# Rotary embedding on the first half of each head: a tile loaded as 11 and 5 rows instead of 8 and 8, and a store released one instruction earlier

## The chip, the core and the metric

The kernel runs on one core of one Trainium2 chip. The metric is device time of one execution in microseconds (us), the median over runs. Three runs of the kernel before were timed: 161.6, 161.76 and 161.9 us. Beside them stands one profiled execution of the same kernel, from which all durations in this text come.

## What is computed

The input `x` has the shape 16 x 512 x 16 x 64 (batch, sequence, heads, dim), in float32: 33.55 MB. `cos` and `sin` are tables of 512 x 32. Of the 64 numbers of a head only the first 32 change, and of the tables only the first 16 columns are used:

```
x1, x2 = x[..., :32], x[..., 32:]
rotated_first  = x1[..., :16] * cos[..., :16] - x1[..., 16:] * sin[..., :16]
rotated_second = x1[..., :16] * sin[..., :16] + x1[..., 16:] * cos[..., :16]
out = concatenate([rotated_first, rotated_second, x2], axis=-1)
```

The second half of each head is copied as it is. So all 33.55 MB are read from HBM and 33.55 MB are written.

## The kernel before, in words

**Tiles.** The 8192 rows of `x` (one row is a batch and sequence position, 16 heads x 64 numbers, 4 KB) are cut into four tiles of 128 partitions x 16 rows: a partition holds 64 KB of a tile, and a whole tile is 8.39 MB. In the code `K` is 16, `KC` is 8 (half a tile) and `KM` is 5. The tiles live in `ring`, which has three slots (`NS`), so tile 3 takes the slot of tile 0 and its load must wait until the store of tile 0 has landed. A tile is loaded into its slot, changed in place and stored from there; the half that isn't rotated travels along.

**Tables.** `cos` and `sin` come by two small DMAs from GpSimd's queue (L63, L64); VectorE spreads them to all partitions (L73 to L83).

**Compute.** All arithmetic is on VectorE. `rotate(t, lo, hi)` works on the rows lo to hi of tile t with four instructions: a product with sin into `b_t` (L96), a product with cos in place (L97), a subtraction for the first 16 columns (L98) and an addition for the second 16 (L101). The tiles are done in order; tile 0, 1 and 3 in two calls of 8 rows; tile 2 as rows 8 to 16, then 0 to 5, then 5 to 8.

**Queues.** The order of transfers is written out by hand. SyncE's queue (SP) issues, in this order: load of tile 0, load of tile 1, load of rows 8 to 16 of tile 2, store of tile 0, load of rows 0 to 8 of tile 2, load of tile 3, store of tile 1, store of tile 3. Only the store of tile 2 is issued by GpSimd (POOL). An instruction of SP that waits holds back those behind it. In what follows "store(0)" is the store of tile 0, and so on; "the first part" and "the second part" of tile 2 are its two loads in their order in time (rows 8 to 16 and rows 0 to 8 here).

**The added wait.** store(1) doesn't wait for tile 1 alone. A dependency added by hand (`tc.add_manual_dep`) lets it wait also for `near`, the last instruction of `rotate(2, 0, KM)`, that is the addition L101 of the rows 0 to 5 of tile 2.

The lines `load` L55 and `store` L58 are helpers, so every load has the line L55 and every store L58 in the profile.

Of the kernel before, what the change touches and what calls it, by code (L numbers as in the profile page):

```python
# [1 line left out]

# [4 lines left out]


@with_exitstack
def kernel(  # L10
    ctx: ExitStack,
    tc: tile.TileContext,
    x: bass.AP,
    cos: bass.AP,
    sin: bass.AP,
    out: bass.AP,
):
    nc = tc.nc
    fp32 = mybir.dt.float32
    P = 128  # L20
    B, S, H, D = x.shape
    Q = D // 4
    HF = D // 2

    K = 16
    T = B * S // (P * K)
    PB = S // K
    REP = P // PB  # L30
    R = H * D
    NS = 3
    KC = K // 2
    KM = 5

    xf = x.rearrange("b s h d -> (b s h d)").rearrange("(t p f) -> t p f", t=T, p=P)
    of = out.rearrange("b s h d -> (b s h d)").rearrange("(t p f) -> t p f", t=T, p=P)
    cosf = cos.rearrange("(p k) j -> p (k j)", k=K)
    sinf = sin.rearrange("(p k) j -> p (k j)", k=K)

    const_pool = ctx.enter_context(tc.tile_pool(name="const", bufs=1))
    b_pool = ctx.enter_context(tc.tile_pool(name="bp", bufs=1, space=bass.MemoryType.PSUM))


    ring = const_pool.tile([P, NS, K, H, D], fp32)
    stage = const_pool.tile([P, 2, K, HF], fp32)
    spun = const_pool.tile([P, 2 * K, Q], fp32)
    packed = const_pool.tile([PB, 2 * K, Q], fp32)
    table = const_pool.tile([P, 2, K, 2, Q], fp32)

    def rows(t, lo, hi):
        return ring[:, t % NS, lo:hi].rearrange("p k h d -> p (k h d)")

    def load(t, lo=0, hi=K):
        return nc.sync.dma_start(out=rows(t, lo, hi), in_=xf[t, :, lo * R : hi * R])  # L55

    def store(t, lo=0, hi=K, queue=nc.sync):
        return queue.dma_start(out=of[t, :, lo * R : hi * R], in_=rows(t, lo, hi))  # L58


    nc.vector.memset(stage[:, :, :, 0:Q], 0.0)  # L61
    spread = stage.rearrange("(j b) t k i -> j b t (k i)", b=REP)
    nc.gpsimd.dma_start(out=spread[:, 0, 0], in_=cosf)  # L63
    nc.gpsimd.dma_start(out=spread[:, 0, 1], in_=sinf)  # L64
    load(0)
    load(1)
    load(2, KC, K)

    PQ = PB // REP
    nc.vector.stream_shuffle(  # L73
        out=spun[:],
        in_=stage.rearrange("p t k j -> p (t k) j")[:, :, 0:Q],
        mask=[j % PQ * REP for j in range(PB)],
    )
    for q in reversed(range(REP)):
        n = PQ * (q + 1)
        nc.vector.tensor_copy(out=packed[0:n], in_=spun[q * PB : q * PB + n])  # L80

    for r in range(REP):
        nc.vector.tensor_copy(  # L83
            out=table[r * PB : (r + 1) * PB].rearrange("p t k c j -> p (t k) c j"),
            in_=packed.unsqueeze(2).to_broadcast((PB, 2 * K, 2, Q)),
        )
    C = table[:, 0].rearrange("p k c j -> p k (c j)")
    Sn = table[:, 1].rearrange("p k c j -> p k (c j)")

    def rotate(t, lo, hi):  # L90
        x1 = ring[:, t % NS, lo:hi, :, 0:HF]
        c = C[:, lo:hi].unsqueeze(2).to_broadcast((P, hi - lo, H, HF))
        s = Sn[:, lo:hi].unsqueeze(2).to_broadcast((P, hi - lo, H, HF))
        b_full = b_pool.tile([P, KC, H, HF], fp32, name="b_t")
        b_t = b_full[:, 0 : hi - lo]
        nc.vector.tensor_mul(out=b_t, in0=x1, in1=s)  # L96
        nc.vector.tensor_mul(out=x1, in0=x1, in1=c)  # L97
        nc.vector.tensor_sub(  # L98
            out=x1[:, :, :, 0:Q], in0=x1[:, :, :, 0:Q], in1=b_t[:, :, :, Q:HF]
        )  # L100
        return nc.vector.tensor_add(  # L101
            out=x1[:, :, :, Q:HF], in0=x1[:, :, :, Q:HF], in1=b_t[:, :, :, 0:Q]
        )

    rotate(0, 0, KC)
    rotate(0, KC, K)
    store(0)
    load(2, 0, KC)
    load(3)
    rotate(1, 0, KC)  # L110
    rotate(1, KC, K)
    behind_loads = store(1)
    rotate(2, KC, K)
    near = rotate(2, 0, KM)
    rotate(2, KM, KC)
    store(2, queue=nc.gpsimd)

    tc.add_manual_dep(
        behind_loads.ins,
        near.ins.name,  # L120
        mybir.DependencyInfo(mybir.DependencyClass.Sync, mybir.DependencyReason.DATA),
        reason="the store follows the loads at the DMA engines",
    )
    rotate(3, 0, KC)
    rotate(3, KC, K)
    store(3)


# [1 line left out]
_INS = ['x', 'cos', 'sin']  # L130
_OUTS = [((16, 512, 16, 64), 'float32')]


# [23 lines left out]
```

## Time and profile before

| what | value | where from |
| --- | --- | --- |
| median of three timed runs | 161.76 us (161.6 to 161.9) | the times |
| span of the profiled execution, first to last instruction | 159.5 us | the page's first line |
| outside of that span, by the median | 2.3 us | 161.76 - 159.5 |
| VectorE (DVE) busy | 112.9 us, 71% of the span | part 1 of the page |
| moved by DMA | 67.24 MB, 422 GB/s over the span | part 2 and 3 |
| HBM read and written | 33.69 MB and 33.55 MB | part 3 |

The profiled execution isn't among the timed ones and has no time of its own beside its span, so the 2.3 us around the span are the difference to the median, taken as unchanged by the edit.

How to read it: the page gives shares of the span; the timeline lists instructions with start and duration, DMA issues among them (an engine name with a q behind it is the engine's sequencer, which issues); the view by windows gives, for any stretch of time, the busy time of each engine, the granted TensorE clock, the DMA share and the GB/s. In this last view a DMA packet (the piece of one partition's row, up to 64 KB, that one of the 16 DMA engines moves) counts with its whole duration and size at its start. So a stretch can show a share over 1, or 0 while all 16 engines work; a stretch in which 16 packets start and that is about one packet long shows a share near 1. The share times the length of the stretch is the time those packets took, per engine.

### The profile page before, as it was taken

The page shows a single profiled execution, that of the slowest core. Times are in us where ns is not written, and L with a number is a line of the kernel's source. Part 1 is how long each engine was busy: PE and PEld are TensorE (multiplying, and loading weights), DVE is VectorE, ACT ScalarE, POOL GpSimd, SP SyncE. Part 2 cuts the span into 40 slices and gives each one's busy share as a digit, 9 for nine tenths or more (in the row PEclk, how much of TensorE's full clock was granted, in tenths as well). Part 3 has the DMA queues.
Part 4 walks back from the last instruction along what each step waited for, and adds up shares of the span by engine and source line. Part 5 has one row for each costly group of instructions (what it writes and reads, how often), then busy time and mean ns, then how long its engine had stood idle before and what let it go on. Part 6 is the DMA issues. An engine that isn't in the chain of part 4 may idle for free.

```text
span 159.5 us, 115 instructions
## 1 busy us (share of the span) xinstructions
DVE 112.9 (71%) x47; POOL 1.9 (1%) x7
## 2 busy tenths in 40 slices
DVE  1000959999999999999999999999999990000000
POOL 3000000000000000000000000010000000000000
DMA  7969979799699699699996996996996997999966
GB/s 263 542 263 542 444 345 526 345 444 526 271 493 551 279 510 526 263 394 411 510 526 263 526 526 263 526 526 263 526 526 263 526 460 329 526 394 394 526 263 263
DMA packets 1360, 67.24 MB, mean 422 GB/s; under 512 B 176, under 2 KB 176, under 8 KB 208
## 3 DMA queue, kind: packets, MB, share of 16 engines
q1 hardware_dynamic: 1152, 58.72, 85.7%
q0 software_dynamic: 208, 8.52, 12.4%
HBM read 33.69 MB, written 33.55 MB: 422 GB/s over the span
## 4 chain that ended last, share of the span: by engine, by line
DVE 61%; DMA 14%; issue 5%; DVEq 1%
DVE b_t L96 22%; DVE ring L97 22%; DMA ring<-in_x_dram 14%; DVE ring L101 10%; DVE ring L98 7%; DVEq L152 1%; DVEq L96 0%
## 5 line engine op out<-in xcount | busy, mean ns | idle before, releaser
L96 DVE TENSOR_TENSOR b_t<-ring,table 128x4096 f32<-128x4096 f32 (+2 forms) x9 | 35.6, 3959 | 2.1 <-DMA ring<-in_x_dram 1.8
L97 DVE TENSOR_TENSOR ring<-ring,table 128x4096 f32<-128x4096 f32 (+2 forms) x9 | 35.5, 3950 | 0.3
L98 DVE TENSOR_TENSOR ring<-ring,b_t 128x2048 f32<-128x2048 f32 (+2 forms) x9 | 18.4, 2049 | 0.3
L101 DVE TENSOR_TENSOR ring<-ring,b_t 128x2048 f32<-128x2048 f32 (+2 forms) x9 | 18.4, 2043 | 0.0
L73 DVE LOAD_MASK_SELECT spun<-stage x1 | 0.0, 14 | 14.4 <-DMA stage<-in_sin_dram 14.4
L83 DVE COPY table<-packed 32x1024 f32<-32x1024 f32 x4 | 2.7, 684 | 0.1
L58 POOL DMA_DIRECT2D out_dram<-ring x1 | 0.6, 562 | 101.7 <-DVE ring L101 101.7
L80 DVE COPY packed<-spun 32x512 f32<-32x512 f32 (+3 forms) x4 | 1.7, 416 | 0.1
L61 DVE MEMSET stage<- 128x512 f32 x1 | 0.5, 485 | 0.9 <-PEq L141 0.9
L73 DVE STREAM_SHUFFLE spun<-stage 128x512 f32<-128x512 f32 x1 | 0.7, 721 | 0.0
L63 POOL DMA_DIRECT2D stage<-in_cos_dram x1 | 0.6, 644 | 1.3 <-DVE stage L61 1.3
L64 POOL DMA_DIRECT2D stage<-in_sin_dram x1 | 0.5, 535 | 0.0
L141 POOL MEMSET const-bfloat16-1.0<- 128x1 bf16 x1 | 0.1, 102 | 0.0
L141 POOL MEMSET const-float32-0.0<- 128x1 f32 x1 | 0.1, 99 | 0.2 <-issue 0.2
L141 POOL MEMSET const-float32-1.0<- 128x1 f32 x1 | 0.1, 99 | 0.0
L141 POOL MEMSET const-uint8-127<- 128x1 uint8 x1 | 0.1, 99 | 0.0
## 6 DMA issues: line engine op xcount, KB each, us to landing
ring<-in_x_dram SPq DMA_DIRECT2D x2, 4096.0 KB, 40.7
stage<-in_cos_dram POOLq DMA_DIRECT2D x1, 64.0 KB, 9.0
stage<-in_sin_dram POOLq DMA_DIRECT2D x1, 64.0 KB, 13.3
ring<-in_x_dram SPq DMA_DIRECT2D x3, 29.0
out_dram<-ring SPq DMA_DIRECT2D x3, 27.4
out_dram<-ring POOLq DMA_DIRECT2D x1, 39.5
```

Source lines behind the costliest of these rows:

```text
L58: return queue.dma_start(out=of[t, :, lo * R : hi * R], in_=rows(t, lo, hi))
L61: nc.vector.memset(stage[:, :, :, 0:Q], 0.0)
L63: nc.gpsimd.dma_start(out=spread[:, 0, 0], in_=cosf)
L64: nc.gpsimd.dma_start(out=spread[:, 0, 1], in_=sinf)
L73: nc.vector.stream_shuffle(out=spun[:], in_=stage.rearrange("p t k j -> p (t k) j")[:, :, 0:Q], mask=[j % PQ * REP for j in range(PB)],)
L80: nc.vector.tensor_copy(out=packed[0:n], in_=spun[q * PB : q * PB + n])
L83: nc.vector.tensor_copy(out=table[r * PB : (r + 1) * PB].rearrange("p t k c j -> p (t k) c j"), in_=packed.unsqueeze(2).to_broadcast((PB, ...
L96: nc.vector.tensor_mul(out=b_t, in0=x1, in1=s)
L97: nc.vector.tensor_mul(out=x1, in0=x1, in1=c)
L98: nc.vector.tensor_sub(out=x1[:, :, :, 0:Q], in0=x1[:, :, :, 0:Q], in1=b_t[:, :, :, Q:HF])
L101: return nc.vector.tensor_add(out=x1[:, :, :, Q:HF], in0=x1[:, :, :, Q:HF], in1=b_t[:, :, :, 0:Q])
L152: with _tile.TileContext(nc) as tc:
```

## The change

Three things are edited.

1. Tile 2 is loaded as rows 5 to 16 (11 rows, before the first store on SP's queue) and rows 0 to 5 (5 rows, behind it). Before, it was rows 8 to 16 and rows 0 to 8.
2. Rows 0 to 8 of tile 2 are rotated as rows 3 to 8 and then rows 0 to 3. Before, it was 0 to 5 and then 5 to 8. The pieces have 5 and 3 rows in both kernels.
3. `rotate` now returns its subtraction and not its addition, so `near`, for which store(1) waits, is the subtraction of rows 3 to 8 of tile 2. The addition follows it on VectorE as before.

```
-    KM = 5
+    KA = 5
+    KM = 3
...
-    load(2, KC, K)
+    load(2, KA, K)
...
-        nc.vector.tensor_sub(
+        first_half = nc.vector.tensor_sub(
...
-        return nc.vector.tensor_add(
+        nc.vector.tensor_add(
             out=x1[:, :, :, Q:HF], in0=x1[:, :, :, Q:HF], in1=b_t[:, :, :, 0:Q]
         )
+        return first_half
...
     store(0)
-    load(2, 0, KC)
+    load(2, 0, KA)
     load(3)
...
-    near = rotate(2, 0, KM)
-    rotate(2, KM, KC)
+    near = rotate(2, KM, KC)
+    rotate(2, 0, KM)
     store(2, queue=nc.gpsimd)
```

No instruction is added or removed on any engine, and each queue issues its transfers in the same order as before. In the changed file each line of `rotate`, `load` and `store` stands one line later (L55 is L56, L98 is L99, L101 is L102).

## The prediction

> **What bounds the kernel now.** I read the page first. VectorE is busy 71% of the span, the DMA row is near full in all but the last slices, and the two DMA queues together hold the 16 engines for 85.7 + 12.4 = 98.1% of the span.
>
> ```profile
> span 159.5 us, 115 instructions
> DMA  7969979799699699699996996996996997999966
> q1 hardware_dynamic: 1152, 58.72, 85.7%
> q0 software_dynamic: 208, 8.52, 12.4%
> DVE 61%; DMA 14%; issue 5%; DVEq 1%
> ```
>
> The last line is the chain that ended last. It runs through VectorE up to the issue of store(3) at 131.2 us, and reads as if VectorE set the end. It does not: store(3) is issued while older stores still keep the DMA engines busy. So the next thing to read is the view by windows around each handover from one transfer to the next, with the issues from the timeline beside it.
>
> ```profile
> 49.92 0.35 SPq L58 DMA_DIRECT2D out_dram<-ring  x1
> 50.31 0.43 SPq L55 DMA_DIRECT2D ring<-in_x_dram  x1
> 71.72 0.33 SPq L55 DMA_DIRECT2D ring<-in_x_dram  x1
> 95.99 1.49 DVE L98 TENSOR_TENSOR ring<-ring,b_t 128x1280 f32<-128x1280 f32 x1
> 97.39 1.48 DVE L101 TENSOR_TENSOR ring<-ring,b_t 128x1280 f32<-128x1280 f32 x1
> 98.90 0.34 SPq L58 DMA_DIRECT2D out_dram<-ring  x1
> ```
>
> These are store(0), the second part of tile 2, load(3), the subtraction and addition before store(1), and store(1).
>
> ```profile
> 1.74:2.60 0.86, 0.00 (x0) 0.86 (x2) 1.00 3.68 1219
> 47.20:49.60 2.40, 2.40 (x2) 0.00 (x0) 1.00 1.01 437
> 50.70:53.10 2.40, 2.40 (x1) 0.00 (x0) 1.00 1.01 437
> 53.10:55.50 2.40, 2.37 (x2) 0.00 (x0) 1.00 1.01 437
> 67.60:70.00 2.40, 2.37 (x2) 0.00 (x0) 1.00 1.15 437
> 70.00:72.50 2.50, 2.47 (x2) 0.00 (x0) 1.00 1.00 419
> 99.50:101.90 2.40, 2.37 (x2) 0.00 (x0) 1.00 1.01 437
> 157.60:159.50 1.90, 0.00 (x0) 0.00 (x0) 1.00 0.00 0
> ```
>
> Columns: the stretch, its length, busy VectorE and GpSimd, clock, DMA share, GB/s. 437 GB/s x 2.40 us is 1.05 MB: 16 packets of 64 KB, one on each engine. In the middle of a transfer (53.10) they take 1.01 x 2.40 = 2.42 us each, so 16 rows of a tile (8 packets an engine) take 19.4 us.
>
> With this the whole span can be added up. 67.1 MB of tiles are 64 packets per engine: 64 x 2.42 = 154.9 us. The tables (0.13 MB) are 0.3 us at the same rate. The first packets take 3.68 x 0.86 = 3.16 us instead of 2.42: 0.7 more. The last packets of store(0) take 1.15 x 2.40 = 2.76 us (0.34 more) and the first of the load behind it 1.00 x 2.50 = 2.50 per 64 KB (0.08 more): a turn from store to load that costs 0.42 us. From a start at about 1.9 us this gives 1.9 + 154.9 + 0.3 + 0.7 + 0.4 = 158.2 us, and the span ends at 159.5 us after the last landing. Nothing is left over for another hole. **The DMA engines bound the kernel, without a gap from the first packet to the last**, and all that can be won at handovers is the 0.42 us.
>
> **The change part by part.**
>
> *The load of 11 rows.* Same bytes in another order. The first part grows by 3 rows: 3/16 of 19.4 = 3.63 us more on the engines ahead of store(0), and 3.63 us less behind it. Sum on the engines: 0. Packets become 44 KB and 20 KB instead of 32 KB, as many as before. Packets of 32 KB run at the rate of 64 KB (the stretch 47.20, in the first part of tile 2, has 1.01 and 437 like the stretch 53.10). 20 KB isn't in the trace; at a loss of 1% on these 6.05 us it would be 0.06 us. I bound it at 0 to +0.1 us and take 0.
>
> What moves: store(0) is still issued at 49.92 us, since tile 0's arithmetic doesn't change, but its turn comes 3.63 us later, at about 54.6 instead of 51.0 us. It is thus queued 4.7 us ahead of its first packet instead of 1.1. It ends 3.63 us later; load(3), which waits on SP for its landing, is issued at 71.72 + 3.63 = 75.3 us. The second part of tile 2 covers this: it is now 5 rows, 6.05 us instead of 9.7, and ends at the old time, about 80.9 us, so load(3) is issued 5.6 us ahead of its turn. Without that cover each us would cost one us. Behind load(3) on SP stand only store(1) (97.5 us) and store(3) (131.2 us), so nothing else is delayed.
>
> VectorE's needs: rows 8 to 16 of tile 2 are used at 76.82 us and land at about 55.7 instead of 52; rows 3 to 8 are used at 90.26 us and the second part lands at 81.3 us as before (issue 50.31 plus 31.0 to landing); tile 3 is used at 104.36 us and lands at 71.72 + 29.0 = 100.7 as before. The nearest of these has 3.6 us to spare. Cost: 0.
>
> *Order 3 to 8, then 0 to 3.* The same shapes in the same places (5 rows, then 3): 0. store(2) on GpSimd waits for the last addition of tile 2, at 104.6 us in both.
>
> *The earlier release of store(1).* The subtraction ends at 95.99 + 1.49 = 97.48 us; the addition ends at 98.87 and the store is issued at 98.90. So store(1) is issued 1.4 us earlier, at 97.5 us. Its turn on the engines is when load(3) ends, from 99.9 us on. What is won is the hole at this handover, and the stretch at 99.50 shows none: 1.01, as in the middle of a transfer. The two decimals of the share allow 0.01 x 2.40 = 0.02 us. Gain 0 to 0.02; behind store(1) on SP nothing is due before 131.2 us. store(2) from GpSimd and store(3) mix with it or follow it on the same busy engines, so the end at about 158.2 us stays.
>
> *How close the cover is.* It matters whether the handovers at 51.0 and 99.9 us have no hole by a wide or a narrow margin. The trace has one start with nothing ahead of it: load(0), issued at 0.74 us. No packet starts before 1.74, and all 16 first packets start from 1.74 to 2.60 us, 1.0 to 1.86 us after the issue.
>
> ```profile
> 0.74:1.74 1.00, 0.48 (x1) 0.03 (x1) 1.00 0.00 0
> 98.90:99.80 0.90, 0.89 (x1) 0.00 (x0) 1.00 0.00 0
> 99.80:100.30 0.50, 0.50 (x1) 0.00 (x0) 1.00 4.86 2097
> ```
>
> store(1)'s 16 first packets start 0.9 to 1.4 us after its issue at 98.90, just when the engines become free. The cover is as long as the delay; a delay of 1.86 us would have left up to 1.86 - 1.0 = 0.9 us of hole. So before the edit both handovers stand at the edge, after it they have 4.7 and 2.4 us. In the profiled execution that is worth 0; in a timed one that falls on the wrong side of the edge it is worth 0 to 0.9 us at each.
>
> Here a rule can be weighed. The Trainium skill, "DMA: Bandwidth & Descriptors", section "Latency and other measured facts", puts the first byte of a transfer issued from SyncE at about 600 ns; the row here is 1.0 to 1.86 us, and the row decides. By the page's figure both handovers would have 0.3 us or more to spare, an earlier issue would be worth nothing in any run, and the sum would be 161.76 us.
>
> *A store queued early behind a load.* This is the state that the trace of before doesn't hold: store(0) issued 4.7 us ahead of its turn, before the engines begin the load's last packets. There is one turn with the following transfer queued long ahead, store(0) to the second part of tile 2 (issued at 50.31, its turn at 70.8 us), and it cost 0.42 us. The two turns from load to store, issued 1.0 us ahead, cost nothing. So the new one costs between 0 and +0.42 us, and from below -0.42 us if the old turn becomes cheaper. I take 0, by the rows with the same direction. store(1), issued at 97.5 us, is only 2.4 us ahead, about one packet: nearer to the rows of 0.
>
> **Sum**: 0 (bytes) + 0 (VectorE) - 0.02 to 0 (store(1)) + 0 (turns) = 159.5 us of span, and with 2.3 us around it 161.7 to 161.8 us. I forecast 161.7 us.
>
> **Rivals.**
> - *Slower: an early store spoils its turn.* If what costs at 70 us is not the direction but that the next transfer lies ready while the last packets run, so that it fetches data beside them, store(0) now pays the same: +0.42, 162.2 us; if store(1) pays too, 162.6 us. For it: the dear turn is the only one queued long ahead. Against it: load to load handovers are queued as long ahead and show no such stretch. It decides once the lead is over one packet, 2.42 us, which store(0) passes and store(1) just reaches. Chance 0.22, and 0.03 more for small packets or another mishap of the same size.
> - *Faster: the timed runs have the holes that the profiled one just misses.* Both handovers are on the edge; 0.4 to 0.5 us at one or both gives 161.3 to 160.8 us. For it: delays up to 1.86 us at load(0). Against it: packets follow without a hole at both handovers here. Chance 0.18.
> - *Faster: the dear turn gets cheaper* as the load behind store(0) has smaller packets: -0.42, 161.3 us. Nothing in the trace speaks for it. Chance 0.04.
> - *The edit does not do what it says*: it moves only what is covered. That is my forecast, chance 0.53.
>
> **Numbers.** A difference of 0.2% (0.32 us) is about what a measurement of this kernel can tell from no change. Faster 0.18 + 0.04 = 0.22, same 0.53, slower 0.22 + 0.03 = 0.25. The likeliest case by itself runs from 161.45 to 162.05 us. The range goes to 161.1 (one hole of 0.65 us closed) and to 162.4 us (one dear turn, and half of another); left out are two full holes and two full dear turns, with about 0.2.
>
> **What would show it.** Right: store(0) issued at 49.9 with its first packets at 54.6; load(3) issued near 75.3; store(1) issued at 97.5; shares near 1.01 at both load to store handovers; the last packets ending near 158.2. Wrong: a share over 1.1 around 54.6 or 99.9 us (early store), or a last packet clearly before or after 158.2 with no such stretch.

## The result and the profile after

The changed kernel takes 162.23 us (median of 6 runs, 162.01 to 163.04); the kernel before took 161.62 us (median of 6 runs, 161.27 to 161.90). The ratio is 1.0045, with a 95% interval of 1.0027 to 1.0062: **slower by 0.45%**. The profiled execution of the changed kernel took 162.12 us with a span of 160.0 us, so what lies around the span is 2.1 us, and the change is inside it: 160.0 against 159.5 us. (The 2.3 us taken for the kernel before came from two different runs; in e1 below one and the same run of it has 161.56 us and a span of 159.5 us, 2.1 us too.)

The page of the changed kernel looks like the one of before:

```profile
span 160.0 us, 115 instructions
DMA  7969979979889969969996996996996997998983
q1 hardware_dynamic: 1152, 58.72, 85.7%
q0 software_dynamic: 208, 8.52, 12.3%
```

The same packets take 85.7 + 12.3 = 98.0% of 160.0 us, which is 156.8 us per engine; before it was 98.1% of 159.5 us, 156.5 us. So most of the 0.5 us is packets that became longer, and not engines that stand idle (a tenth of a per cent is 0.16 us, so the page gives this sum no finer). The timeline of the changed kernel shows the issues (store(0), second part of tile 2, load(3), store(1)):

```profile
49.91 0.35 SPq L59 DMA_DIRECT2D out_dram<-ring  x1
50.30 0.44 SPq L56 DMA_DIRECT2D ring<-in_x_dram  x1
76.24 0.33 SPq L56 DMA_DIRECT2D ring<-in_x_dram  x1
97.50 0.34 SPq L59 DMA_DIRECT2D out_dram<-ring  x1
```

store(0) and store(1) are issued when the prediction said, load(3), which waits for store(0) to land, 0.9 us later than it said (75.3). The view by windows, with each stretch holding the start of one packet per engine, shows where the time is (for the 44 KB packets of the 11 rows, 1.66 us is the time at full rate: 44/64 of 2.42):

```profile
44.40:46.20 1.80, 1.77 (x2) 0.00 (x0) 1.00 0.99 400
46.20:48.00 1.80, 1.80 (x2) 0.00 (x0) 1.00 1.00 400
53.00:54.70 1.70, 1.67 (x2) 0.00 (x0) 1.00 1.32 424
55.30:57.70 2.40, 2.40 (x1) 0.00 (x0) 1.00 1.01 437
72.20:74.60 2.40, 2.37 (x3) 0.00 (x0) 1.00 1.01 437
74.60:75.40 0.80, 0.80 (x1) 0.00 (x0) 1.00 0.97 410
97.40:99.80 2.40, 2.37 (x3) 0.00 (x0) 1.00 1.01 437
```

Three things are to be seen. The **last packets of the 11 rows**, ahead of store(0), take 1.32 x 1.70 = 2.24 us instead of 1.66: 0.58 us too long. Two earlier rounds of 44 KB packets take 0.99 x 1.80 = 1.78 and 1.80 us: 0.26 us too long together. And the turn from store(0) to the load behind it (72.20 and 74.60), which cost 0.42 us before, is now free: 1.01 and 0.97 x 0.80 = 0.78 us where a 20 KB packet takes 0.76. The sum is 0.58 + 0.26 + 0.02 - 0.42 = +0.44 us; the span grew by 0.5. The last 0.1 us is not located. store(1)'s turn (97.40) is at full rate.

### The profile page after: what moved, and what is told of

It reads as the page before. It is cut to its first block, busy times and chain, and to the rows that moved or that the text cites. A ratio compares the mean times of both kernels' runs of the same rounds, so it can differ in the third digit from the quotient of the medians.

```text
span 160.0 us, 115 instructions
## 1 busy us (share of the span) xinstructions
DVE 112.9 (71%) x47; POOL 1.9 (1%) x7
## 3 DMA queue, kind: packets, MB, share of 16 engines
q1 hardware_dynamic: 1152, 58.72, 85.7%
q0 software_dynamic: 208, 8.52, 12.3%
## 4 chain that ended last, share of the span: by engine, by line
DVE 61%; DMA 14%; issue 5%; DVEq 1%
DVE b_t L97 22%; DVE ring L98 22%; DMA ring<-in_x_dram 14%; DVE ring L102 10%; DVE ring L99 7%; DVEq L154 1%; DVEq L97 0%
## 5 line engine op out<-in xcount | busy, mean ns | idle before, releaser
L98 DVE TENSOR_TENSOR ring<-ring,table 128x4096 f32<-128x4096 f32 (+2 forms) x9 | 35.6, 3950 | 0.3
L99 DVE TENSOR_TENSOR ring<-ring,b_t 128x2048 f32<-128x2048 f32 (+2 forms) x9 | 18.4, 2049 | 0.3
L102 DVE TENSOR_TENSOR ring<-ring,b_t 128x2048 f32<-128x2048 f32 (+2 forms) x9 | 18.4, 2043 | 0.0
```

The costliest lines, as they stand in the source:

```text
L99: first_half = nc.vector.tensor_sub(out=x1[:, :, :, 0:Q], in0=x1[:, :, :, 0:Q], in1=b_t[:, :, :, Q:HF])
L102: nc.vector.tensor_add(out=x1[:, :, :, Q:HF], in0=x1[:, :, :, Q:HF], in1=b_t[:, :, :, 0:Q])
```

## The experiments

All ratios are to the kernel before, run beside it on the same chip, with 95% intervals. A "round" is 16 packets, one per engine. "Excess" is a round's time in the view by windows less its time at full rate (2.42 us for 64 KB). The "lead" of a store is the time from its issue to the start of the last packets of the load ahead of it. Theories have letters; those that came up later are told in the expectation in which they first stand.

Theory A: a store that lies ready in the queue well ahead of its turn stretches the last packets of the load before it. Rivals: B, packets of 44 KB are slow by themselves; C, chance disturbances; D, the earlier store(1) costs.

**e1 and e2: both kernels again, unchanged.**

> The kernel before, run again, for a second trace. Theory A (a transfer that lies ready behind another of the other direction stretches that one's last packets): the last packets of store(0), from 68 us on, are again 0.3 to 0.4 us longer than 2.42 us, at the same place, and nothing else is long. Theory C (the long packets are chance disturbances of the memory that fall anywhere): the long packets stand elsewhere or are missing. Time: 161.6 us in both, ratio 1.000 within 0.002.

> The changed kernel, run again. Theory A: the last packets of the 11 rows, from 53.3 us on, are again 0.5 to 0.6 us longer than 1.67 us, and the turn at 74.9 us is free again. Theory B (packets of 44 KB are slow by themselves): the packets from 43 to 48.5 us take about 1.8 us again, 0.3 us in all. Theory C: neither comes back at its place. Time by A and B: ratio about 1.004; by C within 0.002 of 1 or scattered.

e1: 161.54 us, ratio 0.9999 (0.9990 to 1.0008). e2: 162.05 us, ratio 1.0035 (1.0022 to 1.0047). In e1 the last packets of store(0) are again long (share 1.17 where it was 1.15); in e2 the last packets of the 11 rows are:

```profile
52.90:54.60 1.70, 1.67 (x2) 0.00 (x0) 1.00 1.33 424
```

That is an excess of 0.60 us at the same place (0.58 in the first trace of the changed kernel), and the two rounds at 44.4 to 48 us have shares of 0.96 and 1.00 (0.2 us). C falls: the long packets belong to the program.

**e3 and e4: each part of the change alone.** e3 has the loads of 11 and 5 rows and the new order of the pieces, and store(1) waits for the addition (the edit is against the changed kernel):

```
-        first_half = nc.vector.tensor_sub(
+        nc.vector.tensor_sub(
...
-        nc.vector.tensor_add(
+        return nc.vector.tensor_add(
...
-        return first_half
```

e4 has the kernel before with only the subtraction returned:

```
+        first_half = nc.vector.tensor_sub(
...
+        return first_half
```

> The loads of 11 and 5 rows alone; the second store waits for the addition as before. Theory A and B: the whole loss stays, ratio 1.003 to 1.005, with last load packets of 2.2 us at 53 to 56 us. Rival D (the earlier issue of the second store is what costs): ratio within 0.001 of 1.

> The earlier release of the second store alone; loads of 8 and 8 rows. Theory A and B: ratio within 0.001 of 1, the issue of the second store at 97.5 us and no long packet at 99.9 us. Rival D: ratio 1.003 to 1.005, long packets at the end of load(3), 97.5 to 100.5 us.

e3: 162.15 us, ratio 1.0035 (1.0023 to 1.0048). e4: 161.79 us, ratio 1.0012 (1.0003 to 1.0021). The view by windows of e3, then of e4:

```profile
52.90:54.60 1.70, 1.67 (x2) 0.00 (x0) 1.00 1.48 424
```

```profile
67.60:70.00 2.40, 2.37 (x2) 0.00 (x0) 1.00 1.24 437
97.20:99.60 2.40, 2.37 (x3) 0.00 (x0) 1.00 1.04 437
```

The split alone has the whole loss (excess 0.86 us here; its 44 KB rounds at 44.4 to 48 us have shares of 0.94 and 0.96, only 0.1 us too long together). D falls as the main cause. But e4 isn't quite free, as A had expected: store(1), issued at 97.68 us, stretches the last packets of load(3) by 1.04 x 2.40 - 2.42 = 0.08 us. In its trace the old turn is longer too, 0.56 us instead of 0.34 in store(0)'s last packets, but that excess lies between 0.27 and 0.41 us in e1, e5, e10 and e11, which have the same rows ahead of this turn, so a part of it may be chance.

**e5 and e10: a store that lies ready much earlier, in the kernel before.** e5 leaves the added wait out, so store(1) is issued at 76.72 us; e10 waits for an earlier piece, and issues it at 90.27 us. e5, then e10:

```
-    tc.add_manual_dep(behind_loads.ins, near.ins.name, ...)
```

```
-    rotate(2, KC, K)
-    near = rotate(2, 0, KM)
+    near = rotate(2, KC, K)
+    rotate(2, 0, KM)
```

> The kernel before without the added wait: store(1) is issued at about 76.8 us, 23 us ahead of its turn behind load(3). Nothing else is changed. Theory A1 (each turn from load to store whose store lies ready before the last load packets start costs 0.5 to 0.8 us): the last packets of load(3), from 97.5 us on, are 0.5 us or more longer than 2.42, and the ratio is 1.003 to 1.005. Theory A2 (only the first turn with a transfer lying ready costs, about 0.4 to 0.6 us in all, wherever it stands): no long packet at 97.5 us, the one at 68 us stays, ratio within 0.001 of 1.

> The kernel before, with store(1) waiting for rows 8 to 16 of tile 2 instead of rows 0 to 5: it is issued at about 90.3 us, 7 us (three packets) ahead of the last packets of load(3), between the kernel before (98.9 us) and the one without the wait (76.7 us, 1.17 us lost). Step: the last packets of load(3) are again 1.1 to 1.2 us too long, ratio 1.005 to 1.007. Price by the lead: 0.5 to 0.9 us, ratio 1.002 to 1.004.

e5: 162.48 us, ratio 1.0062 (1.0049 to 1.0075). e10: 162.86 us, ratio 1.0083 (1.0069 to 1.0097). The last packets of load(3) in e5, then in e10:

```profile
97.10:99.50 2.40, 2.37 (x3) 0.00 (x0) 1.00 1.50 437
```

```profile
97.10:99.50 2.40, 2.37 (x3) 0.00 (x0) 1.00 1.51 437
```

Both are 1.2 us too long (1.50 x 2.40 = 3.60), where the kernel before has none; in e5 that is more than the 0.5 to 0.8 us expected, and A2 (only the first turn costs) falls. Nothing else differs from the kernel before but the moment of one issue, so this is theory A by itself: 14 us more of lead cost no more, so the price doesn't grow with the lead out here. It also tells what the added wait is for. The time of e10 is above its expected 1.005 to 1.007, though its stretch is no longer than that of e5; why is open.

**e6: the change's loads with store(0) held back.** The 11 and 5 rows stay; store(0) waits for a product that ends when the last load packets start (`rotate` also returns its products for that):

```
+    at_turn = rotate(1, 0, 6)[0]      # the product with sin
+    rotate(1, 6, KC)
...
+    tc.add_manual_dep(first_store.ins, at_turn.ins.name, ...)
```

> The changed kernel with its loads of 11 and 5 rows, but store(0) is held back until about 53.3 us, when the last load packets start, by a wait for a product of tile 1 (whose first call is cut into 6 and 2 rows for that). Theory A1: the long packets at 53.3 us go from 0.6 to under 0.1 us; the turn from store(0) to the load behind it, at 75 us, then costs 0.4 us as in the kernel before; the 44 KB packets at 45 to 48 us stay long (0.2 us); ratio about 1.001 to 1.002. If only what lies ready counts at any turn (theory A as it was), the same. If the turn at 75 us stays free, its cost in the kernel before came from its packets of 32 KB, and the ratio is about 0.999. Rival E (the place, not the lead, makes the last packets long): still 0.6 us at 53.3 us, ratio 1.004.

```profile
46.20:48.00 1.80, 1.80 (x2) 0.00 (x0) 1.00 1.01 400
52.90:54.60 1.70, 1.67 (x2) 0.00 (x0) 1.00 0.99 424
71.50:73.90 2.40, 2.37 (x2) 0.00 (x0) 1.00 1.03 437
```

store(0) is issued at 53.24 us, and the stretch ahead of it is gone (0.99 x 1.70 = 1.68 us); the slow 44 KB packets at 46 us stay. So the lead, and not the place or the packets' size, makes the last packets long. The turn at 73 us costs 0.05 us, where A1 had expected 0.4. The profiled execution has a span of 159.4 us, but the times scatter: 161.65 us (161.25 to 163.32, 12 runs), ratio 1.0021 (0.9997 to 1.0044). Ten runs lie between 161.25 and 162.13 us, two at 163.2 and 163.3. By its time e6 is inconclusive.

**e7: no packets of 44 KB.** The 11 rows are loaded by two DMAs:

```
-    load(2, KA, K)
+    load(2, KA, KC)
+    load(2, KC, K)
```

> The changed kernel, with its 11 rows loaded by two DMAs of 3 rows (12 KB packets) and 8 rows (32 KB packets), so that no packet has 44 KB; store(0) lies ready as early as in the changed kernel. Theory B (packets of 44 KB are slow by themselves): the 0.2 us at 45 to 48 us go. Theory A1: the last packets ahead of store(0) are still 0.5 us or more too long, so the ratio is 1.002 to 1.003 where the changed kernel has 1.004. Rival F (the stretch at the turn belongs to 44 KB packets too): no stretch, ratio below 1.001.

```profile
45.50:46.70 1.20, 1.17 (x1) 0.00 (x0) 1.00 1.01 437
53.30:54.60 1.30, 1.26 (x2) 0.00 (x0) 1.00 1.53 403
```

The 32 KB packets at 45 us run at full rate; the last ones ahead of store(0) take 1.53 x 1.30 = 1.99 us instead of 1.21, an excess of 0.78 us. This agrees with B on the 0.2 us, and F (the stretch belongs to 44 KB packets) falls. The time, 162.50 us, ratio 1.0057 (1.0045 to 1.0069), is above the expected 1.002 to 1.003. The stretch is 0.2 us larger than in the changed kernel, but that only makes up for the 0.2 us won at 45 to 48 us; where the other 0.3 us are wasn't found.

**e8: the load behind store(0) held back**, in the kernel before, until the last packets of store(0) have started.

```
+    at_turn = rotate(1, KC, 13)[1]
+    rotate(1, 13, K)
...
+    tc.add_manual_dep(second_part.ins, at_turn.ins.name, ...)
```

> The kernel before, with the second load of tile 2 held back until about 69.1 us, when the last packets of store(0) have started (tile 1's second call is cut into 5 and 3 rows for that, and store(1) waits for the subtraction of 6 rows, at about 99.0 us). Theory A (what lies ready stretches the last packets of the transfer before): the 0.4 us at 68 to 71 us go, ratio 0.997 to 0.998. Theory G (the 0.4 us are the time that the first reads of a load need behind a store, which a later issue can't shorten): they stay 0.4 us or grow, as a hole instead of long packets, ratio 1.000 to 1.003.

```profile
67.60:70.00 2.40, 2.37 (x2) 0.00 (x0) 1.00 1.01 437
70.00:72.60 2.60, 2.56 (x3) 0.00 (x0) 1.00 1.16 403
```

Issued at 69.10 us, the load no longer stretches the packets of store(0) (1.01), but its own first two rounds take 1.16 x 2.60 = 3.02 us instead of 2.42: 0.60 us lost instead of 0.42. Theory A as it stood ("of the other direction", either way) falls. G (the first reads of a load behind a store need this time) is right that a later issue saves nothing, though the time shows as long packets and not as the hole that G expected. **The two turns are not alike**: in the kernel before and in e8, time is lost from store to load whether the load lies ready or not; from load to store, it is lost only if the store lies ready early. The time, 161.94 us, ratio 1.0023 (1.0015 to 1.0032), holds also a store(1) issued at 99.49 instead of 98.90 us: its first packets start after 100.3 us, where the kernel before had them start from 99.8 to 100.3.

**e9, e17 and e18: the lead in steps.** The changed kernel with KA = 7, 6 and 4, that is 9, 10 and 12 rows ahead of store(0).

```
-    KA = 5
+    KA = 7        # e9; 6 in e17, 4 in e18
```

> The changed kernel with 9 and 7 rows instead of 11 and 5: the turn to store(0) comes 1.2 us later than in the kernel before instead of 3.6 us, so store(0) lies ready less than one packet of 36 KB (1.36 us) before the last packets start. Theory A1 with a step (any store that lies ready before the last packets start costs the whole 0.6 us or more): last load packets 0.6 us too long, ratio 1.003 to 1.004. Theory A1 with a price by the lead (0.6 us at 3.5 us ahead of the last packets, 1.2 us at 21 us): 0.1 to 0.3 us, ratio 1.000 to 1.002. The packets of 36 KB show whether only 44 KB is slow: 0 or about 0.1 us at 41 to 50 us.

> The changed kernel with 10 and 6 rows: store(0) is issued about 1.9 us ahead of the last load packets (40 KB, 1.5 us each), between 9 rows (0.8 us ahead: no stretch) and 11 rows (3.6 us ahead: 0.6 us). Price that grows with the lead: the last packets before store(0) are 0.2 to 0.4 us too long, ratio 1.001 to 1.003. Step at about one packet of lead: 0.6 us or more, ratio 1.003 to 1.004.

> The changed kernel with 12 and 4 rows: store(0) is issued about 4.7 us ahead of the last load packets (48 KB, 1.8 us each). Price that levels off at half the time of a last packet, as the 1.2 us of the 64 KB packets of load(3): 0.8 to 0.95 us, ratio 1.004 to 1.006. Price of 0.6 us whatever the size: 0.6 us, ratio 1.003 to 1.004.

The last packets of the first part, in e9 (36 KB, 1.36 us at full rate), e17 (the last two rounds, 40 KB, 1.51 us) and e18 (48 KB, 1.81 us):

```profile
50.40:51.80 1.40, 1.40 (x1) 0.00 (x0) 1.00 0.98 421
69.00:71.40 2.40, 2.40 (x1) 0.00 (x0) 1.00 1.04 437
```

```profile
50.20:51.70 1.50, 1.50 (x1) 0.00 (x0) 1.00 1.46 437
52.10:53.70 1.60, 1.60 (x1) 0.00 (x0) 1.00 1.23 410
```

```profile
53.70:55.60 1.90, 1.87 (x2) 0.00 (x0) 1.00 1.55 414
```

| kernel | store issued | last load packets start, about | excess ahead of the store |
| --- | --- | --- | --- |
| before, store(0) | 49.92 us | 50.1 us | 0 |
| e6, store(0) | 53.24 us | 53.5 us | 0 |
| e4, store(1) | 97.68 us | 97.8 us | 0.08 us |
| after, store(1) | 97.50 us | 98.1 us | 0 |
| e9, 9 rows | 50.04 us | 51.3 us | 0 |
| e17, 10 rows | 49.80 us | 52.9 us | 1.1 us, over two rounds |
| after, e2, e3, 11 rows | 49.9 us | 53.5 us | 0.58, 0.60, 0.86 us |
| e7, 3 and 8 rows | 50.04 us | 53.9 us | 0.78 us |
| e18, 12 rows | 50.04 us | 54.3 us | 1.1 us |
| e10, store(1) | 90.27 us | 97.5 us | 1.2 us |
| e5, store(1) | 76.72 us | 97.5 us | 1.2 us |

e17: 162.53 us, ratio 1.0061 (1.0046 to 1.0076). e18: 162.47 us, ratio 1.0057 (1.0040 to 1.0074). e9's last load packets start from 51.1 to 51.7 us (none starts from 50.32 to 51.08), so its lead is 1.3 us and not the 0.8 us of the expectations. It is a **step**: up to 1.3 us of lead, about one packet of e9, costs at most 0.08 us; 3.1 us and more cost 0.6 to 1.2 us. No run lies between (of e17's 3.1 us, 0.7 are its own stretch in the round before). So no run tells whether the step sits at a packet's length or at the delay from issue to first packet, which was 0.9 to 1.86 us in the kernel before. Above the step the price follows neither the lead nor the packet's size (0.78 us at 32 KB, 1.1 at 40 KB, 0.6 at 44 KB). So e9 (0) and e18 (1.1 us) lie outside both values that were expected for each, and why the change's own 11 rows get off cheapest stays open.

e9 has neither cost in its trace: nothing ahead of store(0), and 1.04 x 2.40 - 2.42 = 0.08 us at the turn to load. Yet its runs spread from 161.37 to 163.61 us (median 161.82), ratio 1.0033 (1.0012 to 1.0055).

**e11 and e12: can both turns be made cheap?** e11 loads the 8 rows behind store(0) as 5 and 3 rows; e12 is e6 with the 11 rows loaded as 3 and 8 (the edit of e7).

```
-    load(2, 0, KC)
+    load(2, 0, KM)
+    load(2, KM, KC)
```

> The kernel before, with the 8 rows behind store(0) loaded by two DMAs of 5 rows (20 KB packets) and 3 rows (12 KB). Theory H (the turn from store to load is cheap where the load's packets are small, as at 75 us in the changed kernel and in the one with a late store(0)): the 0.35 us at 68 to 72 us fall under 0.1 us, ratio 0.998. Theory I (it is cheap there because of what came ahead of it, not because of its packets): 0.3 to 0.5 us stay, ratio 1.000 to 1.001.

> The kernel with the late store(0) at about 53.2 us, its 11 rows loaded by DMAs of 3 and 8 rows: neither 44 KB packets nor an early store. Theories A1, B and H together: no stretch over 0.1 us at any turn, 0.2 us less at 45 to 48 us than with 44 KB packets, ratio 0.997 to 0.999, the best of all. If a further DMA costs something by itself, up to 1.001.

e11: 161.97 us, ratio 1.0033 (1.0021 to 1.0045). The last packets of store(0) are still 0.27 us too long, so H (small packets make this turn cheap) falls, and I (what came ahead makes it cheap) is left:

```profile
67.90:70.30 2.40, 2.40 (x1) 0.00 (x0) 1.00 1.12 437
```

The time of e11 is above what either expected (1.001 at most); its trace, of a run of 161.77 us, doesn't show why.

e12: 163.16 us (161.66 to 163.82), ratio 1.0088 (1.0055 to 1.0121), the worst and not the best. Its ten runs fall into two groups, four from 161.66 to 161.97 us and six from 162.92 to 163.82; the trace is of a 161.73 us run and shows no stretch at 53 us (share 1.01 over 1.20 us).

**e13 to e16: the kernels with long runs once more**, e12's (e13, e14), e9's (e15) and e6's (e16), one run each.

> The kernel of e12 (late store(0), 3 and 8 rows) once more. Its runs lay in two groups, near 161.7 and near 163.5 us, and the trace at hand is of the first. If this one is of the second group: theory J (store(0) sometimes still lies ready before the last load packets start, and stretches them) shows its 1.8 us as long packets at 53 to 56 us; theory K (the small packets of the first part stall) at 42 to 45 us; theory L (a hole at another turn) at 75 or 99 us.

> The kernel of e12 once more, as in e13, to have a trace of each of its two groups; theories J, K and L expect the same of it as there.

> The kernel of e9 (9 and 7 rows) once more; its runs spread from 161.4 to 163.6 us and the trace at hand is of a short one (161.6). Theory J: in a longer run the excess is in the last packets of 36 KB, at 50.5 to 53 us. Theory L: at another turn.

> The kernel of e6 (late store(0), 11 and 5 rows) once more; two of its 12 runs were near 163.2 us, the others near 161.6. Short: as e6, no stretch at 53.3 us. Long: by J the stretch is back at 53.3 to 56 us, by L it stands at another turn.

They took 161.68, 161.85, 161.66 and 161.68 us: all are short. What the 1.8 us of the long runs are is not known, and theories J, K and L stay untested.

No version beats the kernel before: of the kernels timed with an interval none lies below 1 with it.

## Why the prediction was wrong, point by point

- **The bound held.** The DMA engines have work from first to last packet in both kernels, and VectorE's waits moved nothing.
- **The step that failed is "a store queued early behind a load"**, put at 0 in the sum ("I take 0, by the rows with the same direction"); it cost 0.58 us, and 0.60 and 0.86 us in e2 and e3. Those rows had the right direction but not the state that the edit makes: store(0) was issued as the last load packets started, store(1) 1.3 us after that. e5 and e10 put that state into the kernel before, by one issue alone, and show 1.2 us; e6 takes it out of the changed kernel, and its 0.58 us go from the trace. The rival "an early store spoils its turn" named what happened, but its point of decision (a lead over one packet, 2.42 us, counted to the store's own first packets) was low: by this count e9 has 2.7 us and store(1) of the changed kernel 3.0, and both lost nothing; e17, with 5.1, paid. Its 0.42 us came from the wrong row: e8 shows that this turn has another cause. That it named 162.2 us is luck: it counted one new cost of 0.42 us, and what came was 0.58 + 0.26 us of costs and 0.42 us won at the old turn.
- **The turn behind store(0) was not foreseen to become free.** The prediction gave that 4% for the smaller packets. It did become free (0.42 to 0.02 us), but e11 shows that packet size isn't why. In the traces store(0)'s last packets are at most 0.1 us too long after 9 rows and more, and 0.27 us or more after 8 (in e8 it is the load's first packets). One might think that a store which got ahead during the load's last packets ends its fetching earlier and so hides the load's first reads; but e6, e9 and e12 have the cheap turn without any stretch ahead of the store. The cause stays open.
- **The packets' new sizes** were put at 0 ("I bound it at 0 to +0.1 us and take 0"), with an eye on the 20 KB ones. The 20 KB were right (0.02 us), the 44 KB cost 0.26 us, and 0.1 us in e3 with the same loads. This term was also too small.
- **The early release of store(1)** was right: 97.50 us, no stretch in the changed kernel. By itself (e4) it is at the edge: 0.08 us.
- **The holes at the edge** (rival "faster") were not there: no kernel with a longer lead was faster.

The Trainium skill, "DMA: Bandwidth & Descriptors", section "Rules for kernel authors", advises to issue a DMA early and wait for it late, to overlap it with compute. For the loads here that agrees (load(1) and the first part of tile 2 are issued by 2.1 us at no visible cost); for a store behind a load e5 and e10 speak against it, at 1.2 us. The same page, section "Two DMAs through the same engine are not ordered", says that an engine's read and write sides are separate queues. That would let an early store read from SBUF while the load's last packets are being written there, which is what a stretch of just these packets looks like. No run here shows the two sides apart.

What stays open: the size of the stretch between 0.6 and 1.2 us, the cause of the cheap turn after 9 rows and more, and the long runs of e6, e9 and e12. Because of the long runs, e6 shows by its trace, and not by its time, that holding the store back removes the stretch.

## What to carry to other kernels

When transfers saturate the DMA engines, moving an issue is not free just because all bytes stay the same: look at the last packets ahead of each change of direction. A store behind a load is best issued about when the load's last packets start; 1.3 us after that start it still left no hole here (store(1) in the kernel before), 1.7 us after it left one (store(1) in e8), and 3.1 us or more ahead of it cost 0.6 to 1.2 us. And a cost read off one turn (store to load) is no price for the other (load to store) until a run has made that other state.

## What the runs showed of the hardware that was not expected

- The cost of a store's lead over the load's last packets is a step: 0 at 1.3 us, 0.6 to 1.1 us at 3.1 to 4.3 us, 1.2 us at 7 and at 21 us.
- Of the first parts, those loaded with 9 or 11 rows at once had slow packets at 43 to 49 us: 0.1 to 0.4 us in all with 11 rows (least in e3, most in e16), 0.1 to 0.2 us with 9. With 8, 10 and 12 rows no round at 42 to 49 us was more than about 0.02 us too long. The 3 rows of e12 lost 0.2 us or more at 42 to 44 us, the same 3 rows in e7 less than 0.1. Whether it is the size, where the rows begin or something else was not tried.
- Kernels whose store(0) was issued at most 1.3 us ahead of the last load packets and which loaded 9 or 11 rows ahead of it had runs up to 2.2 us apart: in two groups in e12 and e6, spread from 161.37 to 163.61 us in e9. The kernel before, with 8 rows and a lead of 0.2 us, stayed within 161.1 to 162.1 us in all its runs.
